# Attention heads on one core: where the last score multiplication and the first half's norm stand on VectorE

## The chip, the core and the metric

The kernel runs on one core of a Trainium2 chip. A core has five engines, each with its own queue of instructions, which it takes in order: TensorE (PE; its weight loads have a row of their own, PEld), VectorE (DVE), ScalarE (ACT), GpSimd (POOL) and SyncE (SP), of which SP and POOL only issue DMAs here. The engines wait for each other by semaphores. The working memories are SBUF and the eight PSUM banks that TensorE writes.

The metric is the device time of one execution in microseconds, as the median of several runs.

## What is computed

Two layers of a diffusion backbone over 512 latent tokens (`x`) and 256 context tokens (`ctx`), width 1024. Layer 0 is a bidirectional retention mixer with four heads, layer 1 a gated MLP. The change lies in layer 0. Cut to what matters there:

```python
def retention_chunkwise(q, k, v, log_g, state0):
    ...
        scores = jnp.einsum('bhid,bhjd->bhij', qb, kb) * intra
        o = jnp.einsum('bhij,bhjv->bhiv', scores, vb) + jnp.einsum('bhid,bhdv->bhiv', qb * q_decay, s)
    ...

def retention_output(o, z, w_out):
    o = o * lax.rsqrt(jnp.mean(o * o, axis=-1, keepdims=True) + NORM_EPS)
    b, h, l, dv = o.shape
    o = o.transpose(0, 2, 1, 3).reshape(b, l, h * dv).astype(z.dtype)
    return (o * jax.nn.silu(z)) @ w_out
```

Each head has 256 query and key features and 512 value features. The kernel computes the recurrence as attention without softmax: all scores of a head are multiplied by a matrix of decays (`dt`) and then by the values; the result of each token is normed by the root of its mean square, gated by `silu(z)` and projected to width 1024.

## The kernel before, in words

**Number format.** A float32 operand is split into a high and a low half (`split`: ScalarE copies the high half, VectorE subtracts to get the low one), and a product is three matmuls (`mm3`): low by high, high by low, high by high. So each operand that is made on the chip costs one ScalarE and one VectorE instruction before TensorE can use it.

**Stages.** The projections of layer 0 run first, to about 345 us of the profile. Then the four heads follow, each as `attend` (loads, scores, values, norm) and `project_out` (output projection into `acc`). Layer 1 begins with `prepare` in the last head's projection. In the profile the attends begin near 346, 395, 447 and 497 us.

**One attend.** There are six steps (`steps`): token half `hf` 0 and 1 (256 tokens each), by key blocks `j` = 0, 2, 4 (two blocks of 128 keys each; 0 and 2 are latent tokens, 4 is context). The loop over `i` runs eight times:

- `score(hf, j)`, for i < 6: 12 matmuls of keys by queries into a PSUM bank (`pst`, from two banks with the tag `tm`), then on VectorE `pf` = scores times decay, on ScalarE `ph` = high half, on VectorE `pl` = low half.
- `pv` of the step before last (`LAG` = 2): 12 matmuls of `pl`/`ph` by the values into `po[hf]`, two PSUM banks for the half's 256 tokens.
- When a half's last `pv` is emitted, `finish(hf)` follows: on ScalarE two sums of squares (`junk`, `ss`), a table load and a square root; on VectorE the reciprocal of `ss` and two `gt`, the normed and gated values of 128 tokens each.
- `flip` (at i = 6 for the first half, in `project_out` for the second): eight transposes of `gt` by TensorE into two banks, and `split` of these into `og`, which the output projection reads.
- The side works, one piece for each call of `aside`: `qs` (`load_qk` of the next head: loads, then splits of the `qk` tiles by `halves`), `vs` (`load_v`, from i = 5), `wo` (`load_wo`: loads and splits of this head's output weights, `raw` to `hl`; five pieces) and `step` (sums for the modulation, `ada_a`).

**What sets the order.** TensorE's instructions keep the order of the text (`pe.kept`). VectorE's and ScalarE's are placed by a scheduler that may hoist what is ready, except where the wrapper `Queue` (lines 38 to 64) adds order-only dependencies: in `aside` each instruction is pinned behind the one emitted before it, and `fence()` makes every instruction of that queue that is emitted later come behind the one emitted last:

```python
    def fence(self):
        self.last = self.recent
...
            before = self.recent if self.pinned else self.last
            if before is not None:
                self.tc.add_manual_dep(ins, before.name, NOSYNC, reason="order of the text")
```

DMA loads go through `sp` (`load`), spills to DRAM through GpSimd's queue (`spill`). The tiles `pf`, `ph`, `pl`, `gt` and `junk` share a pool of eleven buffers of 128x512 (`t2`). Nearly all instructions carry line 54 (the wrapper's call), so the profile is read by tile names.

Of the kernel before, what the change touches and what calls it, by code (L numbers as in the profile page):

```python
# [67 lines left out]
def hybrid_kernel(ctx, tc, xT_d, cT_d, cv_d, sv_d, rows_d, ada0_d, adag_d, w_d, rope_d, dec_d, ws_d, id_d, out_d):  # L68
    nc = tc.nc
    pe, act, dve, sp = (Queue(tc, e) for e in (nc.tensor, nc.scalar, nc.vector, nc.sync))  # L70
# [11 lines left out]
    def st(shape, tag, dt=F32, bufs=1, name=None):  # L82
        return sb.tile(shape, dt, tag=tag, name=name or tag, bufs=bufs)
# [34 lines left out]
    def t2(name, shape=(P, 512), dt=F32):  # L118
        return st(list(shape), "t2", dt, bufs=T2, name=name)

    def pt(shape=(P, 512), tag="ps"):
        return ps.tile(list(shape), F32, tag=tag, name="pst", bufs=6 if tag == "ps" else 2)
# [3 lines left out]
    def mm3(out, l, r, first, last):  # L126
        (lh, ll), (rh, rl) = l, r
        mm(out, ll, rh, start=first, stop=False, skip_group_check=True)
        mm(out, lh, rl, start=False, stop=False, skip_group_check=True)
        mm(out, lh, rh, start=False, stop=last, skip_group_check=True)  # L130

    def split(hl, src, late=None):
        h, l = hl
        act.copy(h, src)
        low = lambda: dve.tensor_tensor(l, src, f32(h), ALU.subtract)
        if late is None:
            low()
        else:
            late.append(low)
# [4 lines left out]
    def load(dst, src):  # L144
        sp.dma_start(dst, src)
# [667 lines left out]
    def aside(work):  # L813

        act.pinned = dve.pinned = True
        r = next(work, None)
        act.pinned = dve.pinned = False
        return r

    def step():  # L820
        return aside(bg)
# [35 lines left out]
    def load_qk(h):  # L857
        tags = ("s0", "s1", "s2", "s3", "w4") if h % 2 == 0 else ("rope", "w5", "w6", "g2", "g3")
        srcs = (k_d[h][0], q_d[h][0], k_d[h][1], kc_d[h], q_d[h][1])
        t = []  # L860
        for tag, src in zip(tags, srcs):
            t.append(st([P, 2, 2, HS], tag, F32R, name="qk"))
            load(f32(t[-1][:, 1]).rearrange("p a b -> p (a b)"), src)
            if len(t) % 2:
                yield
        for x in t:
            halves(x)
            yield
        qk[h] = (t[1], t[4]), (t[0], t[2]), t[3]
        yield  # L870
# [3 lines left out]
    def load_wo(h):  # L874
        raws = []
        for c in range(4):
            for j in range(len(raws), min(c + 2, 4)):
                raws.append(st([P, 1024], ("w0", "w7")[j % 2], name="raw"))
                load(raws[j], w_d[16 * h + 12 + j])
            if c == 0:  # L880
                yield
            w = hl_tile()
            split((w[:, 0, :], w[:, 1, :]), raws[c])
            wos.setdefault(h, []).append(w)
            yield
# [3 lines left out]
    def load_v(h):  # L889
        v = []  # L890
        for tag, src in zip(("oA11", "oS1", "oS2"), (*v_d[h], vc_d[h])):
            v.append(st([P, 2, 2, 512], tag, F32R, name="v"))
            load(f32(v[-1][:, 1]), src)
            yield
        z = st([P, NT, 512], "oA12", name="z")
        for t in range(2):
            load(z[:, 2 * t:2 * t + 2, :], z_d[h][t])
        yield
        for x in v:
            halves(x)  # L900
            yield
        vv[h] = v, z
        yield
# [44 lines left out]
    def attend(h, qs, vs):  # L948
        q, k, kc = qk.pop(h)
        v, z = vv.pop(h)  # L950
        dt = dts[h]
        og = [st([P, 2, 4, HS], tag, F32R, name="og") for tag in ("oS3", "oS4")]
        steps = [(hf, j) for hf in range(2) for j in range(0, NK, 2)]
        ph, po, pend = {}, {}, []

        def key(j):
            return (k[j // 2], j % 2) if j < NT else (kc, j - NT)

        def score(hf, j):

            p = pt(tag="tm")
            for o in range(2):
                src, jj = key(j + 1 - o)
                for m in range(2):
                    l = (src[:, 0, m, jj * P:jj * P + P], src[:, 1, m, jj * P:jj * P + P])
                    mm3(p[:, o * HS:o * HS + HS], l, (q[hf][:, 0, m, :], q[hf][:, 1, m, :]), m == 0, m == 1)
            j1 = j + 1
            s0 = hf * HS - P * j1 + P * (NT - 1) if j < NT else XW + hf * HS - P * (j1 - NT) + P * (NC_T - 1)
            base = dt[:, s0:s0 + HS]
            both = bass.AP(base.tensor, base.offset, [base.ap[0], (P, 2), (1, HS)])  # L970
            two = lambda x: x.rearrange("p (o t) -> p o t", o=2)
            a = t2("pf")
            dve.scalar_tensor_tensor(two(a), two(p), 1.0 / 16.0, both, ALU.mult, ALU.mult)
            hl = t2("ph", dt=F32R), t2("pl", dt=F32R)
            split(hl, a)
            ph[hf, j] = hl

        def pv(hf, j):
            if j == 0:
                po[hf] = [pt(), pt()]  # L980
            h, l = ph.pop((hf, j))
            src = v[j // 2]
            for jj in range(2):
                for t in range(2):
                    o = (1 - jj) * HS + t * P
                    mm3(po[hf][t], (h[:, o:o + P], l[:, o:o + P]), (src[:, 0, jj, :], src[:, 1, jj, :]),
                        j + jj == 0, j + jj == NK - 1)
            if j == NK - 2:
                finish(hf)

        def finish(hf):
            ss = st([P, 2], "ss", bufs=2)
            for t in range(2):
                act.activation(t2("junk"), po[hf][t], AF.Square, accum_out=ss[:, t:t + 1])
            act.activation(ss, ss, AF.Sqrt, bias=eps, scale=1.0 / 512)
            dve.reciprocal(ss, ss)
            gts = []
            for t in range(2):
                g = t2("gt")
                dve.scalar_tensor_tensor(g, po[hf][t], ss[:, t:t + 1], z[:, 2 * hf + t, :], ALU.mult, ALU.mult)  # L1000
                gts.append(g)
            pend.append((hf, gts))

        def flip():
            hf, gts = pend.pop(0)
            for fp in range(2):
                pq = pt()
                for b in range(2):
                    for t in range(2):
                        o = b * HS + t * P  # L1010
                        pe.transpose(pq[:, o:o + P], gts[t][:, (2 * fp + b) * P:(2 * fp + b) * P + P], ident)
                src = pq.rearrange("p (b t) -> p b t", b=2)
                split((og[hf][:, 0, 2 * fp:2 * fp + 2, :], og[hf][:, 1, 2 * fp:2 * fp + 2, :]), src)

        LAG = 2
        wo = load_wo(h)
        for i in range(len(steps) + LAG):
            if i < len(steps):
                score(*steps[i])
            if i >= LAG:  # L1020
                pv(*steps[i - LAG])
            aside(qs)
            if i > 4:
                aside(vs)
            if i == len(steps):
                flip()
            if (h, i) == (0, 2):
                sp.pinned = True
                for c in range(4):
                    load(acc[:, 2 * c:2 * c + 2, :], xT_d[:, 2 * c:2 * c + 2, :])  # L1030
                sp.pinned = False
            if i < 5:
                aside(wo)
            if i in (3, 5, 6):
                step()
        return og, flip
# [27 lines left out]
    for h in range(HEADS - 1):  # L1064
        qs, vs = load_qk(h + 1), load_v(h + 1)
        og, flip = attend(h, qs, vs)
        project_out(wos.pop(h), og, flip, (decay(h + 1), vs, qs))
    og, flip = attend(HEADS - 1, iter(()), iter(()))
    for _ in bg:
        pass  # L1070
# [408 lines left out]
```

## Time and profile before

| | us |
|---|---|
| median of 3 runs | 896.98 |
| the runs | 898.55, 896.89, 896.98 |
| the profiled execution | 898.68 |
| its span | 896.90 |
| mean granted TensorE clock | 0.997 |

In the profile's rows `out<-in` names the tiles that an instruction writes and reads, followed by partitions x elements and how many instructions a row merges. A bracket at the end gives the idle time of that engine before the instruction and what ended it. SPq is SP's queue. Ends of matmuls are modelled, so an interval on TensorE is best read from start to start.

### The profile page before, as it was taken

The numbers are of one execution on the slowest core, as the hardware profiler recorded it, in microseconds if no ns is written. First come the engines' busy times: TensorE is split into PE (matmuls) and PEld (weight loads), VectorE is DVE, ScalarE is ACT, GpSimd is POOL, SyncE is SP. The second block draws the span as 40 slices with busy tenths as digits, with TensorE's granted clock in tenths as the row PEclk, the third lists the DMA queues.
The fourth block names the chain that finished last, engine by engine and source line by source line (L and its number), as shares of the span: only waits on it lengthen the run. The fifth ranks groups of instructions, "written<-read, shape, count | busy, mean of one in ns | idle before, by whom it ended". The sixth has DMA issues, their size and how long they took to land.

```text
span 896.9 us, 16938 instructions
## 1 busy us (share of the span) xinstructions
PE 881.9 (98%) x6884; PEld 839.2 (94%) x6884; DVE 712.7 (79%) x996; ACT 461.2 (51%) x717; POOL 51.5 (6%) x88
## 2 busy tenths in 40 slices
PE   8999999999999999999999999999999999999997
PEld 7899999999999999998989999999999899899986
DVE  2689967699679877877678568999888578688995
ACT  5464644444355534636365438744666446356434
POOL 0001211001101101000000001010000000000000
PEclk9999999999999999999999999999999999999999
DMA  9933968457477448747445421545334235136212
GB/s 334 403 126 107 301 216 260 142 177 242 144 251 239 145 160 329 267 137 253 147 130 176 142 70 62 183 165 192 130 119 166 69 118 179 33 118 211 75 44 94
DMA packets 75486, 153.81 MB, mean 171 GB/s; under 512 B 7696, under 2 KB 34448, under 8 KB 75408
## 3 DMA queue, kind: packets, MB, share of 16 engines
q1 hardware_dynamic: 68544, 130.69, 44.0%
q0 software_dynamic: 6720, 22.03, 6.5%
q8 instruction: 54, 0.88, 0.4%
q14 instruction: 24, 0.20, 0.1%
q10 hardware_dynamic: 144, 0.01, 0.0%
HBM read 128.58 MB, written 24.12 MB: 170 GB/s over the span
## 4 chain that ended last, share of the span: by engine, by line
PE 88%; DVE 5%; ACT 3%; DMA 2%; issue 1%; SPq 1%; DVEq 0%; ACTq 0%
PE pst L54 88%; DVE hl L54 2%; DMA xq<-in_xT_dram 1%; DVE raw L54 1%; DMA raw<-in_w_dram 1%; ACT hl L54 1%; ACT junk L54 1%; SPq L54 1%; ACT f L54 1%; ACT oA L54 0%; DVE ada_a L54 0%; DVE pf L54 0%; DVE pl L54 0%; DVE o L54 0%; DVE f L54 0%
## 5 line engine op out<-in xcount | busy, mean ns | idle before, releaser
L54 DVE TENSOR_TENSOR hl<-raw,hl 128x1024 fp32r<-128x1024 f32 x195 | 236.9, 1222 | 79.4 <-ACT hl L54 79.2
L54 ACT CAST hl<-raw 128x1024 fp32r<-128x1024 f32 x195 | 203.6, 1050 | 140.0 <-PE pst L54 68.9
L54 PE MATMUL pst<-hl,oS 128*128 128x256 f32 x1152 | 138.6, 282 | 2.1 <-DVE hl L54 1.9
L54 PEld LDWEIGHTS pst<-hl,oS 128*128 128x128 f32 x1152 | 136.6, 190 | 3.4 <-DVE hl L54 2.1
L54 PE MATMUL pst<-oS,hl 128*128 128x256 f32 x1104 | 133.6, 280 | 0.7 <-ACT oS L54 0.5
L54 PEld LDWEIGHTS pst<-oS,hl 128*128 128x128 f32 x1104 | 130.2, 189 | 2.3 <-ACT oS L54 1.0
L54 PE MATMUL pst<-oA,hl 128*128 128x256 f32 x936 | 117.4, 281 | 0.2
L54 PEld LDWEIGHTS pst<-oA,hl 128*128 128x128 f32 x936 | 112.0, 189 | 2.5 <-issue 1.2
L54 DVE TENSOR_TENSOR raw<-raw 128x1024 f32<-128x1024 f32 x92 | 111.5, 1219 | 1.4 <-DMA raw<-in_w_dram 0.7
L54 ACT COPY snap<-pst 128x512 f32<-128x512 f32 x92 | 53.8, 585 | 104.1 <-PE pst L54 103.7
L54 PE MATMUL pst<-hl,oA 128*128 128x256 f32 x816 | 99.3, 280 | 0.0
L54 PEld LDWEIGHTS pst<-hl,oA 128*128 128x128 f32 x816 | 97.2, 189 | 0.1
L54 PE MATMUL pst<-og,hl 128*128 128x256 f32 x768 | 92.5, 281 | 0.0
L54 PEld LDWEIGHTS pst<-og,hl 128*128 128x128 f32 x768 | 90.4, 189 | 0.9 <-issue 0.2
L54 PE MATMUL pst<-v,ph 128*128 128x512 f32 x192 | 60.1, 395 | 0.0
L54 PE MATMUL pst<-hl,ya 128*128 128x512 f32 (+1 forms) x246 | 59.2, 386 | 0.0
L54 PEld LDWEIGHTS pst<-hl,ya 128*128 128x128 f32 x246 | 45.3, 188 | 9.5
L54 DVE TENSOR_TENSOR snap<-pst,snap 128x512 f32<-128x512 f32 x69 | 47.3, 686 | 5.3 <-PE pst L54 5.1
L54 ACT CAST ph<-pf 128x512 fp32r<-128x512 f32 x24 | 14.9, 621 | 67.3 <-DVE pf L54 66.9
L54 PE MATMUL pst<-hl,hc 128*128 128x256 f32 x384 | 47.1, 279 | 0.0
L54 PEld LDWEIGHTS pst<-hl,hc 128*128 128x128 f32 x384 | 45.6, 189 | 0.0
L54 PEld LDWEIGHTS pst<-v,ph 128*128 128x128 f32 x192 | 36.2, 188 | 7.3
(177 smaller groups left out, 1003.2 us busy)
## 6 DMA issues: line engine op xcount, KB each, us to landing
raw<-in_w_dram SPq DMA_DIRECT2D x224, 256.0 KB, 3.9
bg<-in_adag_dram SPq DMA_DIRECT2D x32, 512.0 KB, 4.3
ada_w<-in_ada_dram SPq DMA_DIRECT2D x16, 512.0 KB, 8.9
raw<-in_w_dram SPq DMA_DIRECT2D x16, 512.0 KB, 4.4
bg<-in_dec_dram SPq DMA_DIRECT2D x12, 512.0 KB, 4.3
v<-snap POOLq DMA_DIRECT2D x16, 256.0 KB, 4.9
z<-snap POOLq DMA_DIRECT2D x16, 256.0 KB, 3.8
v<-v SPq DMA_DIRECT2D x8, 512.0 KB, 4.2
```

Source lines behind the costliest of these rows:

```text
L54: made = op(*args, **kw)
```

## The change

`finish` no longer emits the reciprocal and the gates itself: it puts them, as the new function `gated`, into a list `due`. For the second token half they are taken from it at once, so nothing changes there. For the first half (at i = 4) they are emitted in the next round, behind `score(1, 4)`, the last scores of the head; in that `score` a fence on VectorE behind `pf` puts all that comes later behind it. The round i = 4 ends behind `pv` (`continue`), so its pieces of `qs` and `wo` are emitted in the next round, directly behind the gates. The whole diff:

```diff
@@ -951,7 +951,7 @@
         dt = dts[h]
         og = [st([P, 2, 4, HS], tag, F32R, name="og") for tag in ("oS3", "oS4")]
         steps = [(hf, j) for hf in range(2) for j in range(0, NK, 2)]
-        ph, po, pend = {}, {}, []
+        ph, po, pend, due = {}, {}, [], []
 
         def key(j):
             return (k[j // 2], j % 2) if j < NT else (kc, j - NT)
@@ -971,6 +971,8 @@
             two = lambda x: x.rearrange("p (o t) -> p o t", o=2)
             a = t2("pf")
             dve.scalar_tensor_tensor(two(a), two(p), 1.0 / 16.0, both, ALU.mult, ALU.mult)
+            if due:
+                dve.fence()
             hl = t2("ph", dt=F32R), t2("pl", dt=F32R)
             split(hl, a)
             ph[hf, j] = hl
@@ -993,6 +995,11 @@
             for t in range(2):
                 act.activation(t2("junk"), po[hf][t], AF.Square, accum_out=ss[:, t:t + 1])
             act.activation(ss, ss, AF.Sqrt, bias=eps, scale=1.0 / 512)
+            due.append(lambda: gated(hf, ss))
+            if hf == 1:
+                due.pop(0)()
+
+        def gated(hf, ss):
             dve.reciprocal(ss, ss)
             gts = []
             for t in range(2):
@@ -1017,8 +1024,14 @@
         for i in range(len(steps) + LAG):
             if i < len(steps):
                 score(*steps[i])
+            if due:
+                due.pop(0)()
+                aside(qs)
+                aside(wo)
             if i >= LAG:
                 pv(*steps[i - LAG])
+            if due:
+                continue
             aside(qs)
             if i > 4:
                 aside(vs)
```

## The prediction

> **What bounds the kernel now.** I read the page first: busy times, then the chain that ended last.
>
> ```profile
> PE 881.9 (98%) x6884; PEld 839.2 (94%) x6884; DVE 712.7 (79%) x996; ACT 461.2 (51%) x717; POOL 51.5 (6%) x88
> PE 88%; DVE 5%; ACT 3%; DMA 2%; issue 1%; SPq 1%; DVEq 0%; ACTq 0%
> ```
>
> TensorE (PE) is busy nearly everywhere and carries 88% of the chain. An edit on VectorE (DVE) or ScalarE (ACT) can only gain where PE waits for one of them. So the waits of PE and of its weight loads (PEld) came second: total us, times, longest us.
>
> ```profile
> PEld pst L54 <- DVE pl L54: 1.9, 3, 0.9
> PE pst L54 <- DVE pl L54: 1.2, 2, 0.7
> PEld pst L54 <- DVE og L54: 0.2, 1, 0.2
> ```
>
> `pl` is the low half of the masked scores, and only `attend` writes it: three stalls, in a program with four heads. Third came the timeline of PE at the end of each attend (start, length, engine, what). In every head the eight transposes of the first token half (`pst<-ident,gt`) are followed by the twelve matmuls of `pv(1,4)` and then by the output projection (`og,hl`).
>
> ```profile
> 368.12 1.03 PE L54 MATMUL pst<-ident,gt 128*128 128x128 f32 x8
> 371.99 2.21 PE L54 MATMUL pst<-og,hl 128*128 128x256 f32 x18
> ...
> 417.78 1.04 PE L54 MATMUL pst<-ident,gt 128*128 128x128 f32 x8
> 422.21 0.51 PE L54 MATMUL pst<-og,hl 128*128 128x256 f32 x2
> ...
> 469.07 1.03 PE L54 MATMUL pst<-ident,gt 128*128 128x128 f32 x8
> 473.65 0.52 PE L54 MATMUL pst<-og,hl 128*128 128x256 f32 x3
> ...
> 519.45 1.03 PE L54 MATMUL pst<-ident,gt 128*128 128x128 f32 x8
> 520.24 0.48 PE L54 MATMUL pst<-v,pl 128*128 128x512 f32 x1
> 523.09 5.61 PE L54 MATMUL pst<-og,hl 128*128 128x256 f32 x48
> ```
>
> From transposes to projection the same work takes 3.87, 4.43, 4.58 and 3.64 us in heads 0 to 3. Head 3 shows no stall, so it is the yardstick: the others lose 0.23 + 0.79 + 0.94 = 1.96 us, which agrees with the 1.9 of the weight loads.
>
> [...] By the matmul row the gain would be 1.2 us and the time 895.8; I use the starts.
>
> **Why `pl` is late.** Head 1, from the last scores on:
>
> ```profile
> 410.76 1.58 PE L54 MATMUL pst<-qk 128*128 128x256 f32 x12
> ...
> 413.63 0.30 ACT L54 ACTIVATE ss<-ss,eps 128x2 f32<-128x2 f32 x1
> ...
> 413.95 0.17 DVE L54 RECIPROCAL ss<-ss 128x2 f32<-128x2 f32 x1 [2.08 <-ACT ss L54]
> ...
> 414.16 1.41 DVE L54 SCALAR_TENSOR_TENSOR gt<-pst,ss,z 128x512 f32<-128x512 f32 x2
> ...
> 415.48 0.68 DVE L54 TENSOR_TENSOR qk<-qk 128x512 fp32r<-128x512 f32 x1
> 416.08 1.22 DVE L54 TENSOR_TENSOR hl<-raw,hl 128x1024 fp32r<-128x1024 f32 x1
> 417.22 0.68 DVE L54 SCALAR_TENSOR_TENSOR pf<-pst,dt 128x512 f32<-128x512 f32 x1
> ...
> 417.94 0.62 ACT L54 CAST ph<-pf 128x512 fp32r<-128x512 f32 x1 [2.55 <-DVE pf L54]
> ...
> 418.59 0.69 DVE L54 TENSOR_TENSOR pl<-pf,ph 128x512 fp32r<-128x512 f32 x1 [0.69 <-ACT ph L54]
> 419.20 0.69 DVE L54 TENSOR_TENSOR qk<-qk 128x512 fp32r<-128x512 f32 x1
> ...
> 421.60 1.28 DVE L54 TENSOR_TENSOR og<-pst,og 128x512 fp32r<-128x512 f32 x2
> ```
>
> The scores are in PSUM at 412.34, but `pf` starts at 417.22. VectorE stands idle 2.08 us at the reciprocal, until ScalarE's square root lands, and the gates, one `qk` half and one `hl` half follow before `pf`. Then `pf` to `ph` to `pl` costs another 2.06 us, so PE waits.
>
> **The change, part by part.**
>
> *`pf` ahead of the reciprocal* (the fence and `due`). The built order of VectorE becomes `pf`, reciprocal, `pl`, both `gt`, `qk`, `hl`; on ScalarE the last `ph` now stands directly behind the square root, ahead of `qk` and `hl`. PE's order is unchanged. With head 1's durations: `pf` 412.34 to 413.02, inside the old idle time; root until 413.93; `ph` until 414.55; `pl` until 415.24 instead of 419.28. PE without a stall wants it at 417.78 + 0.79 (the step from transposes to `pl` in head 3) = 418.57. The margin is 3.3 us, so the stalls of heads 0 to 2 go: -1.96.
>
> *The gates become later.* They now run behind `pl`: 415.24 + 1.41 = 416.65, where they ended at 415.57. The transposes start at 417.78, 1.1 us later, and that hides it; without this cover each microsecond would stall PE at the flip. `po[0]`'s banks come free 1.1 us later too; the next user of such a bank is the projection, at 422.21.
>
> *What is late next: `og`.* Behind the gates stood 6.03 us of queue until `og` (415.57 to 421.60); `pf`, the gap and `pl` took 1.98 of it (417.22 to 419.20). Afterwards `og` starts at 416.65 + 6.03 - 1.98 = 420.70, 0.90 earlier than now. PE arrives 0.79 earlier. So the gain of head 1 survives by 0.1 us, and the 0.2 us that it waits for `og` now may stay or go: 0 to -0.2, taken as 0, since the new margin is that thin. Heads 0 and 2 have the same order and more room for it, as head 0's PE moves by only 0.23 and head 2 also loses an `hl_e` there (below).
>
> *Deferred halves and output weights.* At i = 4 nothing is emitted behind `pv`; at i = 5 `qs` and `wo` come behind the gates and `qs` once more behind `pv`. So one `qk` half (ACT about 0.6, DVE 0.68) and the last weight split (DVE 1.22, ACT about the same) keep their count and stand behind `pl` instead of ahead of `pf`. Both are read only in the projection or the next head: 0. The moved pieces issue no DMA: that piece of `wo` only splits, its four loads having been issued before. On the SP queue one pair changes places, in head 1: the next head's second `v` load ahead of one `raw` load that waits for the split. The load is of output weights of the next head, whose attend begins near 447, over 25 us later: 0. On POOL nothing moves. `step` and `vs` lose no turn (`vs` starts at i = 5).
>
> *What the fence drags along.* A fence holds every VectorE instruction that stands later in the text. Before the change the scheduler had hoisted three instructions of the next stage (`prepare` and the first weight sums) into head 2:
>
> ```profile
> 468.89 1.23 DVE L54 TENSOR_TENSOR hl_e<-raw,hl_e 128x1024 fp32r<-128x1024 f32 x1 [0.21 <-ACT hl_e L54]
> ...
> 473.03 1.22 DVE L54 TENSOR_TENSOR raw<-raw 128x1024 f32<-128x1024 f32 x1
> ...
> 490.09 1.23 DVE L54 TENSOR_TENSOR raw<-raw 128x1024 f32<-128x1024 f32 x1 [0.74 <-DMA raw<-in_w_dram]
> ```
>
> They now stand in head 3: `hl_e` between `pf` and `pl`, one `raw` ahead of the gates, one ahead of `og`; 3.68 us in all. Head 3 before:
>
> ```profile
> 512.43 1.58 PE L54 MATMUL pst<-qk 128*128 128x256 f32 x12
> ...
> 514.96 0.17 DVE L54 RECIPROCAL ss<-ss 128x2 f32<-128x2 f32 x1 [2.75 <-ACT ss L54]
> 515.16 1.41 DVE L54 SCALAR_TENSOR_TENSOR gt<-pst,ss,z 128x512 f32<-128x512 f32 x2
> ...
> 516.48 1.22 DVE L54 TENSOR_TENSOR hl<-raw,hl 128x1024 fp32r<-128x1024 f32 x1
> ...
> 520.70 1.29 DVE L54 TENSOR_TENSOR og<-pst,og 128x512 fp32r<-128x512 f32 x2 [1.02 <-ACT og L54]
> ...
> 524.65 0.48 DVE L54 SCALAR_TENSOR_TENSOR acc<-pst,gate,acc 128x256 f32<-128x256 f32 x1 [2.66 <-PE pst L54]
> ```
>
> Following instructions start about 0.08 us before the last one ends (415.48 against 415.57). `pf` 514.01 to 514.69, `hl_e` until 515.84, `pl` until 516.45, reciprocal until 516.6, `raw` until 517.8, gates until about 519.15; PE's transposes start at 519.45. That leaves 0.3 us. Then `hl` until 520.3, `raw` until 521.45, `og` until 522.65, and PE wants the first half of it at 523.09; VectorE is idle before 524.65 anyway, so the debt is paid there. From below the cost is 0. From above: had `pf` no idle time to use, the gates would end at 516.57 + 0.60 + 0.61 + 1.15 + 1.14 = 520.07 and the flip would stall 0.6. I take 0, as `pf`'s input is ready 0.95 us ahead of the reciprocal.
>
> **Sum.** -0.23 - 0.79 - 0.94 + 0 + 0 = -1.96. The profiled execution took 898.68 us with a span of 896.90; it becomes 896.72. But it lies 1.70 above the median of the runs shown, 896.98, which becomes 895.02. I predict 895.0 us. The bounds of the parts give 894.8 (`og` wait gone too) to 895.6 (head 3 pays 0.6).
>
> **The rivals.**
>
> *The wait moves one step down, to `og`.* If VectorE's queue is no earlier at `og`, PE meets it there: head 1 gives back all its 0.79; head 2, where `og` starts at 471.84 and PE at 473.65, gives back little. Gain 1.17, time 895.8. For it: head 1's margin of 0.1 and its present wait for `og`. Against: the 2.08 idle microseconds that `pf` fills.
>
> *Scatter hides it.* The runs shown are 896.89, 896.98 and 898.55, the profile 898.68: two groups 1.6 us apart. If the median after falls into the upper one: 898.6 - 1.96 = 896.7, not told from before. Nothing in the engines speaks for it, but two of four executions were there. The case that the edit does nothing (the scheduler restoring the old order) is excluded by the built order.
>
> *Head 3 pays (slower).* VectorE runs its queue strictly in order: above, `pf` sat 4.9 us behind a waiting reciprocal. In head 3 `pl`, the gates and `og` now sit behind three foreign instructions, one of which waited 0.74 us for its DMA when it ran at 490.09. If a load of theirs or `hl_e` is late there, all of VectorE stands and the flip waits. It decides as soon as the delay exceeds the 0.3 us of cover; the whole gain is gone at 0.3 + 1.96 = 2.3 us of lateness. With all 3.68 us uncovered the kernel ends at 895.0 + 3.7 = 898.7. Against: those loads had landed by 490, some 24 us earlier, and VectorE's idle 2.75 us takes in most of it.
>
> [...]
>
> **How the numbers follow.** A measurement of this kernel tells about 0.2% from no change: 1.79 us, so below 895.2 counts as faster and above 898.8 as slower. Forecast 0.56; `og` rival 0.14; scatter 0.18; head 3 pays 0.12. The forecast case straddles 895.2: it is faster in nine parts of ten (0.50); its rest, the `og` case and the scatter give 0.38 for the same. The last case lies at 898.7 with all of its price, around the bound; I leave its 0.12 on slower. The range goes from 894.5 (0.3 below the bound, for scatter among runs) to 897.2, past the scatter case and no change; it leaves out the uncovered head 3. The forecast's own range is 894.6 to 895.6.
>
> **What would show it.** Right: no row of PEld waiting for `pl`; `pf` of the last step starting within 0.1 us of the scores' end, ahead of the reciprocal; transposes to projection near 3.64 us in all heads; VectorE's idle time before the reciprocals down from 2.1 us to below 0.5. Wrong: a new wait of PE for `gt` in head 3 or for `og` in heads 1 and 2; `hl_e` or `raw` idle on a DMA in head 3; or a span 1.9 us shorter while the runs do not follow.

## The result and the profile after

| | before | changed |
|---|---|---|
| median of 10 runs each, us | 897.24 | 895.05 |
| lowest and highest, us | 895.42, 898.61 | 893.92, 896.41 |
| profiled execution, us (its span) | 898.68 (896.9) | 895.43 (893.6) |
| first scores of head 0 to last head's projection, us | 177.28 | 175.02 |

The ratio is 0.9978, with a 95% interval from 0.9969 to 0.9988: faster by 0.22%, at the border of what a measurement of this kernel tells from no change. The changed kernel was measured a second time (below): 0.9975, from 0.9963 to 0.9987.

The page after, busy times and the chain that ended last:

```profile
PE 879.8 (98%) x6884; PEld 838.1 (94%) x6884; DVE 712.7 (80%) x996; ACT 461.0 (52%) x717; POOL 51.3 (6%) x88
PE 91%; DVE 4%; ACT 2%; DMA 1%; SPq 0%; issue 0%; DVEq 0%
```

VectorE does as much as before (712.7 us); TensorE carries 91% of the chain instead of 88%. The change took work from nobody; it took waits away. The view of TensorE's waits (us in total, times, longest us) no longer has a row for `pl` or `og`. Behind the program's first microsecond, what VectorE still makes it wait for at length is one thing, outside the heads:

```profile
PE pst L54 <- DVE hl L54: 1.9, 1, 1.9
...
PEld pst L54 <- DVE hl L54: 2.4, 2, 2.1
```

The timeline of TensorE, transposes of the first token half and start of the output projection, heads 0 to 3:

```profile
366.96 1.03 PE L54 MATMUL pst<-ident,gt 128*128 128x128 f32 x8
...
370.60 0.62 PE L54 MATMUL pst<-og,hl 128*128 128x256 f32 x4
...
416.38 1.03 PE L54 MATMUL pst<-ident,gt 128*128 128x128 f32 x8
...
420.02 0.73 PE L54 MATMUL pst<-og,hl 128*128 128x256 f32 x5
...
466.77 1.03 PE L54 MATMUL pst<-ident,gt 128*128 128x128 f32 x8
...
470.40 0.85 PE L54 MATMUL pst<-og,hl 128*128 128x256 f32 x6
...
516.19 1.03 PE L54 MATMUL pst<-ident,gt 128*128 128x128 f32 x8
...
519.83 0.85 PE L54 MATMUL pst<-og,hl 128*128 128x256 f32 x6
```

From start to start that is 3.64, 3.64, 3.63 and 3.64 us: every head now runs as only head 3 did. Head 1 in the timeline of VectorE and ScalarE shows why:

```profile
410.98 0.69 DVE L54 SCALAR_TENSOR_TENSOR pf<-pst,dt 128x512 f32<-128x512 f32 x1 [0.62 <-PE pst L54]
...
412.12 0.30 ACT L54 ACTIVATE ss<-ss,eps 128x2 f32<-128x2 f32 x1
412.32 0.60 ACT L54 CAST ph<-pf 128x512 fp32r<-128x512 f32 x1
412.45 0.17 DVE L54 RECIPROCAL ss<-ss 128x2 f32<-128x2 f32 x1 [0.77 <-ACT ss L54]
...
412.96 0.69 DVE L54 TENSOR_TENSOR pl<-pf,ph 128x512 fp32r<-128x512 f32 x1 [0.34 <-ACT ph L54]
...
413.57 1.41 DVE L54 SCALAR_TENSOR_TENSOR gt<-pst,ss,z 128x512 f32<-128x512 f32 x2
...
419.02 1.28 DVE L54 TENSOR_TENSOR og<-pst,og 128x512 fp32r<-128x512 f32 x2
```

`pf` starts when the scores land and fills most of the idle time in front of the reciprocal (0.77 us are left of 2.08). `pl` ends at 413.65, 3.5 us ahead of its use (its weight load starts at 417.15). The gates end at 414.98, 1.40 us ahead of the transposes. `og` starts 2.64 us behind the transposes' start, where it was 3.82 (421.60 less 417.78), so 1.18 us earlier.

Head 3 has the three instructions that the fence dragged in:

```profile
510.79 0.69 DVE L54 SCALAR_TENSOR_TENSOR pf<-pst,dt 128x512 f32<-128x512 f32 x1 [1.66 <-PE pst L54]
...
511.40 1.22 DVE L54 TENSOR_TENSOR hl_e<-raw,hl_e 128x1024 fp32r<-128x1024 f32 x1
...
513.21 1.21 DVE L54 TENSOR_TENSOR raw<-raw 128x1024 f32<-128x1024 f32 x1
514.33 1.41 DVE L54 SCALAR_TENSOR_TENSOR gt<-pst,ss,z 128x512 f32<-128x512 f32 x2
...
516.78 1.22 DVE L54 TENSOR_TENSOR raw<-raw 128x1024 f32<-128x1024 f32 x1
```

No bracket stands behind `hl_e` or `raw`: neither waited for a load. The gates end at 515.74, 0.45 us ahead of the transposes at 516.19.

The two profiled spans differ by 3.3 us, more than the stalls hold. The rest lies ahead of the heads. First scores of head 0 before, then after:

```profile
345.81 0.63 PE L54 MATMUL pst<-qk 128*128 128x256 f32 x4
```

```profile
344.81 1.57 PE L54 MATMUL pst<-qk 128*128 128x256 f32 x12
```

That microsecond is in code that the change doesn't touch: up to the first scores, TensorE, VectorE and ScalarE run the same instructions in the same order in both kernels. So the experiments are read by the stretch from these first scores to the last head's projection: 345.81 to 523.09 before, 344.81 to 519.83 after, 2.26 us less. The 1.96 of the stalls are in it, and 0.12 that TensorE lost to `og` in head 1 (0.2 in the row of weight loads). The other 0.16 lies ahead of head 0's transposes, 22.31 us from the first scores before and 22.15 after. Neither kernel has a stall there, and the repeat of the kernel before (experiment 5) takes 22.15 too, so it is not the change's. The gain is about 2.1 us.

### The profile page after: what moved, and what is told of

It is laid out like the page before. It is cut to its first block, busy times and chain, and to the rows that moved or that the text cites. A ratio compares the mean times of both kernels' runs of the same rounds, so it can differ in the third digit from the quotient of the medians.

```text
span 893.6 us, 16939 instructions
## 1 busy us (share of the span) xinstructions
PE 879.8 (98%) x6884; PEld 838.1 (94%) x6884; DVE 712.7 (80%) x996; ACT 461.0 (52%) x717; POOL 51.3 (6%) x88
## 4 chain that ended last, share of the span: by engine, by line
PE 91%; DVE 4%; ACT 2%; DMA 1%; SPq 0%; issue 0%; DVEq 0%
PE pst L54 91%; DVE hl L54 1%; DMA xq<-in_xT_dram 1%; DVE raw L54 1%; ACT hl L54 1%; ACT f L54 1%; SPq L54 0%; ACT junk L54 0%; ACT oA L54 0%; DVE o L54 0%; DVE ada_a L54 0%; DVE f L54 0%; DVE oS L54 0%; DVE xq L54 0%; DVE snap L54 0%
```

## The experiments

Unless a diff says otherwise, the edits are made in the changed kernel. "Stretch" is the one just named. Each run without a ratio had one profiled execution.

**1. Gates behind `pf`, side work left where it was** (e1_gates_only).

```diff
             if due:
                 due.pop(0)()
-                aside(qs)
-                aside(wo)
             if i >= LAG:
                 pv(*steps[i - LAG])
-            if due:
-                continue
```

> One half of the change alone: the first half's gates go behind the last pf (with the fence), but the qk half and the last weight split keep their place at i = 4, so VectorE's order is pf, reciprocal, qk, hl, pl, gates. Own theory (what PE waits for at the end of an attend sets the gain): pl ends near 2.4 us before PE wants it, so no wait for pl; but the gates end 1.7 to 1.8 us later than in the changed kernel, behind the start of the transposes, so PE waits for gt at the flip in heads 0 to 2, by 0.3 to 0.7 us each; from transposes to projection 3.64 us everywhere, and about 1.5 us of the gain of 2.0 lost. Rival (the gain is only in moving pf): no wait at all, time as the changed kernel.

Ratio 0.9996 (0.9981 to 1.0011), median 895.61; stretch 176.38, 1.36 us longer than that of the changed kernel. The loss is larger than that. From the first scores to the second half of head 2's projection this execution takes 134.39 us and the changed kernel 131.83: 2.56 us are lost, all of the gain, and the ratio of 0.9996 agrees. From there to head 3's transposes it takes 38.35 us, the changed kernel 39.55, for the same matmuls without a stall (477.83 to 516.18 against 476.64 to 516.19). That is the change of pace told in the last section, and it hides 1.2 us. The view of waits names the new wait:

```profile
PEld pst L54 <- DVE gt L54: 2.6, 4, 1.1
```

The timeline shows it in head 1:

```profile
415.69 1.40 DVE L54 SCALAR_TENSOR_TENSOR gt<-pst,ss,z 128x512 f32<-128x512 f32 x2
416.49 0.14 PEld L54 LDWEIGHTS pst<-ident,gt 128*128 128x128 f32 x1 [1.13 <-DVE gt L54]
416.49 0.33 PE L54 MATMUL pst<-ident,gt 128*128 128x128 f32 x1 [0.70 <-DVE gt L54]
```

With a `qk` half and a weight split still ahead of them, the gates come too late for the flip. The expected 3.64 us from transposes to projection in all heads did not come: they are 3.99, 4.23, 3.92 and 3.64, since the transposes also wait for the second gate. Deferring the side work is therefore a needed part, not an accompaniment.

**2. Side work deferred, gates left ahead of `pf`, no fence** (e2_side_only).

```diff
             due.append(lambda: gated(hf, ss))
-            if hf == 1:
-                due.pop(0)()
+            due.pop(0)()
...
-            if due:
-                due.pop(0)()
+            if i == 5:
                 aside(qs)
                 aside(wo)
...
-            if due:
+            if i == 4:
                 continue
```

> The other half alone: the gates stay ahead of the last pf, without a fence, but the qk half and the last weight split go behind pl, so VectorE's order is reciprocal, gates, pf, pl, qk, hl. Own theory: pf starts about 1.8 us earlier than before (0.68 + 1.22 less the overlap), pl ends about 1.0 us ahead of PE's need, no stall of PE is left: transposes to projection 3.64 us in all heads and the same time as the changed kernel, 2.0 us below before. Rival (the multiplication ahead of the norm is what gains): pl still late, a stall of 0.2 to 0.9 us in heads 0 to 2.

Ratio 1.0001 (0.999 to 1.0012), median 897.27; stretch 176.49, 1.47 us lost (0.16 of them ahead of head 0's transposes, as in the first profile of the kernel before). The first part of the expectation came true: no stall for `pl` is left. The second did not: head 1 now meets the prediction's first rival.

```profile
413.56 0.17 DVE L54 RECIPROCAL ss<-ss 128x2 f32<-128x2 f32 x1 [2.08 <-ACT ss L54]
...
421.47 1.28 DVE L54 TENSOR_TENSOR og<-pst,og 128x512 fp32r<-128x512 f32 x2
...
422.21 1.98 PE L54 MATMUL pst<-og,hl 128*128 128x256 f32 x15 [0.94 <-DVE og L54]
```

VectorE still stands 2.08 us at the reciprocal, its queue is as long as before, and `og` at its end comes no earlier: 4.12 us behind the transposes' start, where it was 3.82. Only an order that puts work into that idle time brings `og` forward. Each half of the change alone moves the wait to another tile; together they remove it.

**3. No fence** (e3_no_fence).

```diff
             dve.scalar_tensor_tensor(two(a), two(p), 1.0 / 16.0, both, ALU.mult, ALU.mult)
-            if due:
-                dve.fence()
```

> The changed kernel without the fence: the scheduler keeps the same order in heads 0 to 2 and in head 3 leaves hl_e and the two weight sums in head 2, so VectorE's order in head 3 is pf, reciprocal, pl, gates. Own theory: same time as the changed kernel within 0.2 us of span behind the first attend, because head 3's gates, at 0.2 us, were just in time; gates in head 3 end some 2 us earlier. Rival (the fence's three instructions cost something): 0.3 us or more below the changed kernel.

Ratio 0.9982 (0.9968 to 0.9995), median 894.3; stretch 175.03 and 3.64 us in all heads. Head 3, without the foreign instructions:

```profile
509.42 0.69 DVE L54 SCALAR_TENSOR_TENSOR pf<-pst,dt 128x512 f32<-128x512 f32 x1 [1.63 <-PE pst L54]
...
511.44 1.40 DVE L54 SCALAR_TENSOR_TENSOR gt<-pst,ss,z 128x512 f32<-128x512 f32 x2
...
516.07 1.29 DVE L54 TENSOR_TENSOR og<-pst,og 128x512 fp32r<-128x512 f32 x2 [2.09 <-ACT og L54]
```

The gates end at 512.84, the transposes start at 514.81: 1.97 us of cover instead of 0.45. The fence spends 1.5 us of cover and buys nothing, as the scheduler keeps `pf` first without it. But spent cover costs no time.

**4. How much cover is there: gates computed two and three times** (e5_gates_x2, e5_gates_x3).

```diff
-                dve.scalar_tensor_tensor(g, po[hf][t], ss[:, t:t + 1], z[:, 2 * hf + t, :], ALU.mult, ALU.mult)
+                for again in range(2 if hf == 0 else 1):
+                    dve.scalar_tensor_tensor(g, po[hf][t], ss[:, t:t + 1], z[:, 2 * hf + t, :], ALU.mult, ALU.mult)
```

For the second run the 2 is a 3.

> The changed kernel with each first-half gate computed twice: 1.33 us more on VectorE ahead of the transposes, in each head. From the changed kernel's profile, gates end 1.4 us ahead of the transposes in head 1 and 0.45 in head 3; the first og half ends 0.99, 0.35, 1.73 and 1.26 us ahead of the projection in heads 0 to 3. Theory (each cover is spent first and what is left stalls PE one to one): head 0 loses 0.3 and head 1 loses 1.0 at og, head 2 nothing, head 3 loses 0.9 at the transposes: transposes to projection 4.0, 4.6, 3.6, 3.6 and the stretch from the first scores to the last head's projection 175.0 + 2.2 = 177.2 us. Rival (the margins are not there, any microsecond ahead of the transposes is paid): 4 x 1.33 = 5.3, stretch 180.3.

> The changed kernel with each gate of the first half computed three times (the same value): 4 more instructions of 0.67 us, 2.7 us later gates in each head. Own theory: the cover of the gates is 1.2 to 1.5 us in heads 0 to 2 and 0.2 us in head 3, so PE stalls at the flip by about 1.2 to 1.5 us in heads 0 to 2 and 2.4 us in head 3, 6 to 7 us in all, plus waits for og behind it of up to 0.5 us. Rival (the gates lie far from the path, any delay is hidden): no stall, time as the changed kernel.

Per head 1.33 and 2.67 us of work were added, 5.3 and 10.7 in all; the stretch grew by 2.55 (to 177.57) and 8.75 us (to 183.77). With two, the timeline shows the wait for `og` in heads 0 and 1, and for the gates in head 3:

```profile
370.06 2.12 PEld L54 LDWEIGHTS pst<-og,hl 128*128 128x128 f32 x18 [0.46 <-DVE og L54]
...
420.76 1.32 PEld L54 LDWEIGHTS pst<-og,hl 128*128 128x128 f32 x11 [1.19 <-DVE og L54]
...
517.17 0.14 PEld L54 LDWEIGHTS pst<-ident,gt 128*128 128x128 f32 x1 [0.53 <-DVE gt L54]
...
517.83 0.75 PEld L54 LDWEIGHTS pst<-ident,gt 128*128 128x128 f32 x7 [0.52 <-DVE gt L54]
```

Expected were 0.3, 1.0, none and 0.9. The weight loads waited 0.46, 1.19 and 0.28 at the flip of head 1, none, and 1.05; from start to start of the matmuls the heads lose 0.42, 1.26, none and 0.86. The sizes are near those expected, the place is not: in heads 0 and 1 the projection starts nearly on time (3.64 and 3.77 us behind the transposes, 4.0 and 4.6 expected) and waits for the second half of `og`. Cover is spent first, and only what exceeds it is paid. (The waits of the weight loads add up to 2.98 us, the losses from start to start of the matmuls to 2.54.) With three, the gates' wait is as expected, `og` takes more, and one thing was in no expectation: behind an idle time of 1.51 and 0.33 us at the flip of head 3, the granted clock falls. The view of waits:

```profile
PEld pst L54 <- DVE gt L54: 6.7, 8, 1.9
...
PEld pst L54 <- DVE og L54: 1.8, 2, 1.2
```

The view by stretches (PEclk is the third number from the end):

```profile
518.00:523.00 5.00, 3.56 (x16) 2.60 (x14) 5.00 (x9) 0.49 (x1) 0.00 (x0) 1.00 0.94 287
523.00:528.00 5.00, 4.60 (x16) 3.74 (x17) 4.14 (x6) 1.17 (x2) 0.00 (x0) 0.66 0.05 16
```

A share of 0.66 over 5 us costs 5 x 0.34 = 1.7 us, an estimate from the share alone. Without it the three-fold gates cost 7.05. Ahead of head 3's flip the matmuls also ran at the quicker pace (40.03 us from 483.05 to 523.08, of which 1.51 idle, against 39.55 without idle time), which hides about 1 us more. So of the first 5.3 us about half was paid (2.55), of the second 5.3 some 4.5 as measured, about 5.5 at equal pace: the cover was used up.

**5. Repeats** (e8_changed_again, e10_before_again: both kernels unaltered).

> The changed kernel once more, unaltered. My reading (a gain of 2.26 us, all of it between the first scores and the last head's projection; the rest of the difference of the two profiled spans is scatter ahead of the heads): the stretch is 175.0 us within 0.1, transposes to projection 3.64 in all four heads, and the ratio to the kernel before lies at 0.9975 within 0.0013. Rival (the start ahead of 345 us has changed too, worth another 1 us): ratio 0.9965 or below, and first scores 1 us earlier than in the profile of before whether the clock falls or not.

> The kernel before once more, for the repeatability of what the gain was read from. My reading: the same waits in the heads (transposes to projection 3.87, 4.43, 4.59, 3.64, each within 0.2) and 177.3 us within 0.15 from the first scores to the last head's projection, whether the clock falls or not (first scores at 345.8 with a fall, near 343.4 without). Rival (the stalls of the first profile were an accident of that execution): the three heads together lose under 1.5 us.

The changed kernel: ratio 0.9975 (0.9963 to 0.9987), stretch 175.03, 3.64 us in all heads. The kernel before: stretch 177.14, with 4.25, 4.13, 4.52 and 3.64 us from transposes to projection. Head 0's and head 1's shares changed by more than 0.2 us against that expectation, but the three heads lose 0.61 + 0.49 + 0.88 = 1.98 us, as in the first profile (1.96). The gain between the repeats is 2.12 us. The first scores of the changed kernel's repeat stand at 343.46, within 0.1 us of two experiments (343.44 and 343.43): the start differs between executions of the same kernel (344.81 in the first profile) by more than the 1.0 us in question, so nothing makes that microsecond the change's.

**6. Where the scatter ahead of the heads comes from.** In every kernel so far TensorE waits once for VectorE at about 222 us, 1.8 to 1.9 us long. It is in the second of the four k and q projections (two expectations below call it the last), where VectorE also has rope and the modulation sums (`step`). In some profiles, not in all, the clock falls there too (the view by stretches: length, busy time and count of PE, PEld, DVE, ACT and POOL, then PEclk, DMA share and GB/s; first the changed kernel, then that without the fence; the last section says why the stretches are cut at these times):

```profile
221.41:224.82 3.41, 1.47 (x13) 1.40 (x13) 3.41 (x4) 1.41 (x2) 0.00 (x0) 1.00 0.53 187
224.82:228.23 3.41, 3.41 (x19) 3.41 (x18) 0.88 (x1) 0.67 (x2) 0.00 (x0) 0.50 0.82 237
```

```profile
222.12:225.53 3.41, 1.87 (x16) 1.87 (x17) 3.41 (x4) 0.93 (x1) 0.00 (x0) 1.00 0.63 191
225.53:228.95 3.42, 3.42 (x32) 3.42 (x32) 1.20 (x2) 1.53 (x2) 0.00 (x0) 1.00 0.82 254
```

In the changed kernel's profile half the clock is granted for 3.41 us: 19 matmuls in place of 32, a loss of 1.7 us by the share. From the end of the wait (223.43 and 223.66) to the first scores the two executions take 121.38 and 119.77 us. Five runs moved turns of `step` in the loop over the projections, by three edits. That of the last pair reads:

```diff
-            if 2 not in pieces and i not in (2, 4):
+            if n not in (2, 5) and 2 not in pieces and (i not in (2, 4) or n in (0, 1, 3, 4, 6)):
                 pieces.append(step())
```

In e6_kq_clear (changed kernel without its fence) and e7_before_kq_clear (kernel before), the turns of the second k and q projection alone are left out there: `n != 2`. In e9_kq_both, those of the second and third: `n not in (2, 5)`. In e11_spread (changed) and e12_before_spread (before), two turns more in each of five other projections make up for them. The sums themselves are complete in all.

> The changed kernel without its fence, and in the last k and q projection (about 205 to 236 us of the profile) no turn of the modulation sums; these come later, so no work is left out. In the profiles so far TensorE waits there 1.8 to 1.9 us at about 222 us for a VectorE that is late, and in some executions the granted clock falls to 0.5 for 3.41 us at about 225 us. Theory (the wait brings the fall of the clock, and the fall the two groups of run times): with the wait gone the clock stays at 1.0 behind 10 us in every execution, the runs lie within 1.5 us, and the median falls by 1.9 (the wait) plus half of 1.7 (the fall, in about half of the executions): 891.5 us against 894.3 of the kernel without the fence. Rival 1 (the scatter comes from the start of the run or the loads): only the wait goes, 892.4 us, and the runs lie 2.9 us apart as before. Rival 2 (the late work only moves): the same wait of PE shows in a later projection, 894 to 895 us. Both theories: the stretch from the first scores to the last head's projection stays 175.0 us.

> The kernel before with the same turns of the modulation sums left out of the last k and q projection (they come later). If the clock's fall hangs on that wait, as in the run before this one, its runs lie within 1.5 us, the median is 2.8 us under the kernel before (893.6 against 896.4), and with the run before this one the change can be measured without the scatter: 2.3 us, from the stretch from the first scores to the last head's projection (177.3 against 175.0). If the scatter has another source: 1.9 under, with the runs still 3 us apart or more.

Ratios 0.9978 (0.9967 to 0.999) and 1.0007 (0.9993 to 1.0021), the runs 2.9 and 6.4 us apart: both expectations failed, and of the rivals the one that the late work only moves was right about the wait. In the first of the two:

```profile
300.81 3.00 PE L54 MATMUL pst<-oS,hl 128*128 128x256 f32 x24 [1.75 <-DVE hl L54]
```

> The changed kernel with no turn of the modulation sums in the second and third k and q projections (about 205 to 236 and 275 to 305 us); the turns come later, nothing is left out. With the second projection alone cleared, the wait of TensorE moved from 222 us (1.94) to 301 us (1.75). Theory (VectorE has room later and the clock's fall follows such a wait): no wait of PE over 0.5 us between 60 and 345 us, clock 1.0 behind 10 us, first scores near 341.6 us (343.45 without a fall, less 1.9), median 891.0 us, runs within 1.5 us of each other. Rival 1 (the backlog moves once more, to the fourth k and q projection or to the heads, where the turns compete with the gates): a wait of 1 to 2 us there, median 893 to 895 us. Rival 2 (the scatter has nothing to do with the wait): median 1.9 less than the changed kernel's, but the runs still lie 3 us apart. The heads themselves: transposes to projection 3.64 in all four, unless rival 1 shows there.

Median 895.39, ratio 0.9987 (0.9974 to 1.0001). No wait over 0.5 us is left between 60 and 345 us, and the first scores start at 341.95; but the heads pay 2.80 us (stretch 177.82), since turns that were put off now end there:

```profile
341.95 4.38 PE L54 MATMUL pst<-qk 128*128 128x256 f32 x36
...
455.61 1.65 PE L54 MATMUL pst<-qk 128*128 128x256 f32 x12 [0.96 <-DVE gateb L54]
```

> The changed kernel with no turn of the modulation sums in the second and third k and q projection, and with two turns more in each of five other projections (two ahead of 205 us, two between 236 and 275, one behind 305), so that the sums are done about when they were and nothing reaches the heads. Theory (the wait of 1.94 us at 222 us goes, no other takes its place, and without it the clock doesn't fall): first scores near 342.0 us, the stretch to the last head's projection 175.0, clock 1.0 behind 10 us, span near 341.95 + 175.0 + 373.8 = 890.8, median 892.2 us or below and runs within 1.5 us of each other, so about 4 us under the kernel before. Rival (the extra turns make another projection wait): PE waits for VectorE between 130 and 345 us again, first scores at 343 or later, median as the changed kernel's, 893 to 895 us.

> The kernel before with the same moved turns. Theory: first scores near 342.0 us as in the run before this one, the stretch to the last head's projection 177.2, so 2.2 us above that run, with runs within 1.5 us of each other: the gain of the change measured without the fall of the clock. Rival (part of the gain of the two first profiles was the clock): the two runs differ by under 1.5 us.

With the turns spread, the wait at 222 us shrinks to 0.42 and nothing else grows; e11_spread's row:

```profile
223.50 2.89 PE L54 MATMUL pst<-hl,oS 128*128 128x256 f32 x23 [0.42 <-DVE hl L54]
```

Its median is 892.05, ratio to the kernel before 0.9966 (0.9949 to 0.9984), the best ratio of all the runs; stretch 175.03, first scores 342.82. The kernel before with the same spread: 893.3, ratio 0.9978 (0.996 to 0.9996). The expected 2.2 us between the two came out as 1.25, and neither was narrow: 888.47 to 894.4 and 889.41 to 896.74. So e11_spread is likely the better version, but its interval overlaps that of the change alone, with which it was not run side by side.

What these runs show of the clock: the mean granted clock of an execution was under 0.998 in 5 of 10 of the changed kernel's runs and 2 of 12 of its repeat, in 13 of the 30 of experiments 1 to 3, and in 8 of 24 of e6 and e7, which have the wait at 301 us. Where no such wait over 0.5 us stands ahead of the heads (e9, e11 and e12) it was so in 0 of 36, while the kernel before, which ran beside them, had it in 12 of 40. So in these runs the lower clock goes with the wait. It is not all of the scatter, since the last pair still spreads over 6 to 7 us.

## Why the prediction held, step by step

- *Stalls for `pl`, -1.96.* Right. All three are gone, in both profiles of the changed kernel, and experiments 1 and 2 show that they went by the mechanism named.
- *The time, 895.0.* Measured 895.05, and that it is so close is luck. The median before was 897.24 in ten runs, not the 896.98 of three, so the runs moved by 2.19 and not 1.96; the two differences cancel. The changed kernel's runs also form two groups, five with a granted clock of 0.996 (895.43 to 896.41, mean 896.01) and five at 0.998 or more (893.92 to 894.68, mean 894.33), and their median stands in the gap between. In the repeat, with 2 of 12 runs at the lower clock and 10 of 29 of the kernel before, the medians lie 3.05 apart.
- *Margin of `pl`, 3.3 us.* Measured 3.5.
- *Gates 1.1 us ahead of the transposes.* Measured 1.40. The chain from the scores' start to `pl`'s end took 4.28 us in place of the 4.48 worked out. Doubling the gates agrees: 1.33 us more left 0.28 of wait at the weight loads there.
- *`og`, taken as 0 between 0 and -0.2.* This was the mis-sized term. `og` came 1.18 us earlier, not 0.90, and the old wait went too, worth 0.12 from start to start. With it the sum is -2.08, against 2.10 (2.26 less the 0.16 of pace) and 2.12 in the two pairs of profiles.
- *Deferred halves and output weights, 0.* Right in the complete change. Experiment 1 priced the alternative: if they stay ahead of the gates, all of the gain is lost (2.56 us at equal pace).
- *What the fence drags along, 0, with 0.3 us of cover.* Right: 0.45 us of cover, no time. Experiment 3 shows that 1.5 us of cover went there.
- *The rival "`og`"* (0.14): not in this change, but it is what its second half alone does (experiment 2, 0.94 us in head 1's matmul row). Both the thin margin and the reason against it, the idle time that `pf` fills, were the right ones.
- *The rival "scatter hides it"* (0.18): the scatter is there, and the two groups after lie 1.68 us apart, as the 1.6 of the prediction had it. What tells them apart, where the prediction found nothing in the engines, is the granted clock: 0.996 in the one, 0.998 or 0.999 in the other (experiment 6). It didn't hide the gain, as five of ten runs stood in the lower group; with all in the upper one the median would have been 896.0.
- *The rival "head 3 pays"* (0.12): neither load nor `hl_e` was late. One addition of 1.33 us ahead of its gates cost 0.86 from start to start, which is what exceeds the 0.45 of cover, so the point from which it decides was real.
- *What would show it:* `pf` started within 0.1 us of the scores' modelled end (410.98 against 409.37 + 1.58). The idle time in front of the reciprocals fell to 0.56, 0.77, 0.26 and none in heads 0 to 3, two of them above the 0.5 foreseen.
- *The profiled execution* was to become 896.72 and was 895.43. The heads gave 0.3 us more than summed, of which 0.16 is pace; 1.0 us is the start, which no step of the change touches.

## What to carry to other kernels

Fill a waiting engine's idle time with the next stage's first link before shortening its queue: in this kernel, work put into the gap moved what stood behind it forward, and work merely swapped in order moved the wait to the next tile. Check each half of such a reordering for the tile that is late next; here `gt` and `og` each took over the wait when one half was left out. When a change is worth 2 us of 900, measure it in the trace over a stretch that excludes scatter from elsewhere, and repeat the profile. Look first whether the matmuls run at the same pace in both: a stretch alone would have put the loss in experiment 1 at about half of what it was.

## What the hardware did that was not expected

*The clock falls after a wait of under 2 us.* One idle time of TensorE of 1.94 us was followed, in some executions and not in others, by 3.41 us at half clock, 1.7 us of time by the share; another one of 1.51 and 0.33 us in experiment 4 too (0.66 over 5 us). The 23 matmuls behind the first take 4.10 us in the changed kernel's profile, 4.21 in that of before and 4.37 in e10_before_again, but 2.89 in e3_no_fence and e8_changed_again, behind the same wait (1.93 us in e10_before_again, 1.94 in the others). The traces of before and changed show where the falls stand. Their record of the granted clock begins 6.75 and 6.37 us into the span, and both falls start 218.45 us behind that, at 225.21 and 224.82. That is 64 times 3.413 us, which is also the length of each of the two. The falls at the programs' ends, where TensorE has finished, start at 894.22 and 890.42 us, 260 and 259 times 3.413 us behind the same beginning. So in these two traces the clock changes only on a grid of 3.413 us; the stretches in experiment 6 are cut by such a grid. The interval ahead of either fall near 225 us has 1.94 us of TensorE's idle time (3.41 less 1.47 in the changed kernel). Among the intervals behind which the two traces keep the full clock, none has over 1.16. In e3_no_fence the author's cut at 222.12 us divides the same wait of 1.94 us, the larger part is 1.54 (the third row of the stretches in experiment 6, 3.41 less 1.87), and no fall came. That the place of the grid settles which executions are hit is the author's reading of these three traces. How much idle time a fall takes is not shown beyond these cases.

*Matmuls change pace at a full granted clock.* From the second half of head 2's projection to head 3's transposes, in the view by stretches, first the changed kernel, then e12_before_spread:

```profile
476.64:516.19 39.55, 39.55 (x279) 36.83 (x278) 26.47 (x41) 14.92 (x23) 0.00 (x0) 1.00 0.49 157
```

```profile
477.18:515.53 38.35, 38.35 (x279) 35.84 (x278) 25.44 (x39) 14.65 (x23) 0.00 (x0) 1.00 0.48 156
```

TensorE is busy throughout in both, at the same PEclk of 1.00 and with the same 279 matmuls, and one takes 1.2 us less. That lowers that run's stretch to 176.53. The same 38.35 us stand in experiment 1, while the kernel before and the other runs without added gates take 39.55 there, so it does not go by the change; whether it goes by the execution is not shown. It may be part of what spreads the runs of the last pair. Its cause was not found.
